# Sixteen row blocks of a down projection by seven block products in place of eight

## Chip, cores, metric

One NeuronCore of a Trainium2 chip runs the whole kernel. The metric is the device time of one execution in microseconds (us); lower is better. Five engines work side by side, each through its own instructions in a fixed order: PE (matrix products), DVE (vector), ACT (scalar and activation), POOL (GpSimd), and SP, which here only issues DMAs. They wait for each other through semaphores.

## What is computed

One layer of a hybrid decoder over 592 columns (16 meta tokens, 512 prompt tokens, 8 sequences of 8 new tokens). A pooling mixer and a state space mixer are merged, projected by w_o and added to x; then comes the channel mixer, which is the part that the change is about:

```python
hn2 = rmsnorm(x, norm2_w)
up, ffn_new = causal_dwconv(hn2 @ w_up, ffn_buf, ffn_conv_w, ffn_conv_b)   # width 3, 5632 columns
x = x + (silu(up[..., :D_FF]) * up[..., D_FF:]) @ w_down                   # D_FF = 2816 = 22 blocks of 128
# then a last rmsnorm of x
```

All of it is float32. Every weight product is made of three matmuls on rounded parts: low weight by high activation, high by high, high by low.

## The kernel before

Activations lie with features on the 128 partitions and tokens in columns. The work is a list of **units**. A unit is one block of 128 output features: it loads a weight block (`load_w`, L87, a DMA on SP into one of two "wr" buffers of 1 MB; one load often serves two units), **splits** it (`split_w`: ACT writes the high part wh at L116, DVE the low part wl at L117, into one of two buffers each, `WBUFS`), does its matmuls (`mm3`, L122 to L124), and ends with a "post" that reads the sums from PSUM. `run` sets the order: after unit u it emits the split of unit u+2, which has to wait for the buffer that unit u has read. A tile scheduler then lays out each engine's instructions in one fixed order by its own costs; within an engine nothing overtakes.

Stages from 580 us on: the merge (units of w_ssd_out, from about 600 us), the output projection (`o_units`; its post sums squares of x2 on POOL and turns the next block of x on PE through an "acc" buffer), the up projection, the down projection, the rest of both. In the up projection the units go gate 0, val 0, gate 1, val 1, ... for j = 0 to 21, 48 matmuls of 290 and 288 columns each. `gate_post` and `val_post` read PSUM (L1157 to L1159), convolve (ACT L1165, DVE L1167 twice), and make tanh (L1179) and its product (L1180) or the product gate times value (L1190), whose high part ACT writes (L1194) and whose low part POOL writes (L1195) into `gh` and `gl`. After j = 11, `down0` multiplies blocks 0 to 11 by w_down: 8 units, two halves of 288 columns, 12 k each, added into x2 by DVE (L1220). After j = 21, `last` does blocks 12 to 21, with the output's transposes between.

Of the kernel before, what the change touches and what calls it, by code (L numbers as in the profile page):

```python
# [8 lines left out]
F32 = mybir.dt.float32  # L9
F32R = mybir.dt.float32r  # L10
# [25 lines left out]
def hybrid_step(  # L36
# [23 lines left out]
    def slot(shape, dt=F32):  # L60
        return sp.tile(shape, dt, tag="T", bufs=9, name=nm("t"))
# [66 lines left out]
    class Unit:  # L128
# [8 lines left out]
        def split(self):  # L137
            if self.ws is None:
                wr = self.raw() if callable(self.raw) else load_w(*self.raw)
                self.ws, k0 = [], 0  # L140
                for kb in self.kbs:
                    w = split_w(wr[:, k0:k0 + kb, self.at:self.at + self.n], kb, self.n, self.spare if kb == 2 else None)
                    self.ws += [(w, k) for k in range(kb)]
                    k0 += kb
                self.pss = []
# [20 lines left out]
        def finish(self):  # L166
# [972 lines left out]
    run(merge[:2] + [ff_params] + merge[2:] + [lambda: xr.extend(load_x(c) for c in range(5))], o_units)  # L1139
    x2s = []  # L1140

    def x2_norm():
        return rnorm(sums["n2"], DM, lambda r, a, b: S.activation(rs2[:, a:b], r, AF.Copy))


    nff, rs2 = slot([128, 18 * 44]), slot([128, NA])

    LF = LP - A0
    WF = LF + 8 * NB
# [2 lines left out]
    def ffn_conv(kb, pss):  # L1152
# [19 lines left out]
        return ap[:, 0:NP], ap[:, 514:594].rearrange("p (b r) -> p b r", b=NB)[:, :, 0:8]  # L1172

    gates = {}
    gh, gl = [], []

    def gate_post(j, pss):
        ext, acc, w = ffn_conv(j, pss)
# [1 line left out]
        V.scalar_tensor_tensor(ext[:, 0:w], ext[:, 0:w], 1.0, acc[:, 0:w], op0=ALU.add, op1=ALU.mult)  # L1180
        gates[j] = ext

    def val_post(j, pss):
        if j % 2 == 0:
            gh.extend(pairs(2, F32R))
            gl.extend(pairs(2, F32R))
        _, acc, w = ffn_conv(NF + j, pss)
        t = gates.pop(j)
        for a, b in zip(parts(t), parts(acc)):
            V.tensor_tensor(a, a, b, ALU.mult)  # L1190
        hi, lo = blk(gh, j)[:, :NY], blk(gl, j)[:, :NY]
        for a, h, l in zip(parts(t), (hi[:, 0:NP], hi[:, NP:].rearrange("p (b j) -> p b j", b=NB)),
                           (lo[:, 0:NP], lo[:, NP:].rearrange("p (b j) -> p b j", b=NB))):
            S.activation(h, a, AF.Copy)  # L1194
            G.tensor_tensor(l, a, f(h), ALU.subtract)  # L1195

    def ff_units(j0, nj):
        out = []
# [120 lines left out]
```

## Time and profile before

| | |
|---|---|
| median of 3 runs | 1229.65 us (1229.41 to 1229.66) |
| profiled execution | 1229.33 us |
| its span, first to last instruction | 1227.6 us |
| mean granted TensorE clock | 0.997 |
| PE busy | 1213.3 us (99%) |
| DVE busy | 778.6 us (63%) |
| ACT busy | 554.3 us (45%) |
| POOL busy | 163.5 us (13%) |

The profile is of one execution. "Busy" of PE counts matmuls that are pipelined, so it says that PE always has work and not that it runs at its peak; whether it waits is read from the chain of waits and from the gaps in the timeline. Clock 1.00 is the full rate.

### The profile page before, as it was taken

The numbers are of one execution on the slowest core, as the hardware profiler recorded it, in microseconds if no ns is written. First come the engines' busy times: TensorE is split into PE (matmuls) and PEld (weight loads), VectorE is DVE, ScalarE is ACT, GpSimd is POOL, SyncE is SP. The second block draws the span as 40 slices with busy tenths as digits, with TensorE's granted clock in tenths as the row PEclk, the third lists the DMA queues.
The fourth block names the chain that finished last, engine by engine and source line by source line (L and its number), as shares of the span: only waits on it lengthen the run. The fifth ranks groups of instructions, "written<-read, shape, count | busy, mean of one in ns | idle before, by whom it ended". The sixth has DMA issues, their size and how long they took to land.

```text
span 1227.6 us, 22630 instructions
## 1 busy us (share of the span) xinstructions
PE 1213.3 (99%) x9159; PEld 1176.5 (96%) x9159; DVE 778.6 (63%) x1378; ACT 554.3 (45%) x1167; POOL 163.5 (13%) x323
## 2 busy tenths in 40 slices
PE   9999999999999999999999999999999999999996
PEld 7999999999999999989999999999999999999996
DVE  6785246668997998886643443477666235667634
ACT  6444443555757567655532223443443112433432
POOL 0340000012012013021100001221212000121100
PEclk9999999999999999999999999999999999999998
DMA  7144425653554545664454432123222223222322
GB/s 213 50 137 128 134 89 181 174 161 80 155 146 124 155 135 154 184 168 118 134 154 123 143 131 98 41 91 96 90 70 78 78 86 104 70 69 91 112 70 77
DMA packets 173432, 144.00 MB, mean 117 GB/s; under 512 B 11622, under 2 KB 162830, under 8 KB 173321
## 3 DMA queue, kind: packets, MB, share of 16 engines
q1 hardware_dynamic: 172865, 142.14, 39.5%
q8 instruction: 72, 1.18, 0.4%
q10 hardware_dynamic: 464, 0.42, 0.1%
q14 instruction: 31, 0.25, 0.1%
HBM read 122.43 MB, written 20.34 MB: 116 GB/s over the span
## 4 chain that ended last, share of the span: by engine, by line
PE 94%; DVE 3%; DMA 1%; issue 1%; ACT 1%; POOL 0%; SPq 0%; DVEq 0%; ACTq 0%; POOLq 0%
PE mm L122 28%; PE mm L123 27%; PE mm L124 27%; PE px L765 2%; PE px L827 1%; PE px L787 1%; PE px L796 1%; PE px L749 1%; DMA wr<-in_w_in_dram 1%; PE px L840 1%; DVE wl L117 1%; PE px L880 1%; PE px L739 0%; DVE ext L561 0%; PE px L122 0%
## 5 line engine op out<-in xcount | busy, mean ns | idle before, releaser
L122 PE MATMUL mm<-s,wl 128*128 128x288 f32 (+4 forms) x2512 | 753.1, 300 | 0.6 <-DVE wl L117 0.6
L123 PE MATMUL mm<-s,wh 128*128 128x288 f32 (+4 forms) x2512 | 746.2, 297 | 0.0
L124 PE MATMUL mm<-s,wh 128*128 128x288 f32 (+4 forms) x2256 | 670.7, 297 | 0.0
L122 PEld LDWEIGHTS mm<-s,wl 128*128 128x128 f32 x2512 | 473.4, 188 | 9.2 <-issue 6.5
L123 PEld LDWEIGHTS mm<-s,wh 128*128 128x128 f32 x2512 | 473.1, 188 | 2.9 <-issue 2.4
L124 PEld LDWEIGHTS mm<-s,wh 128*128 128x128 f32 x2256 | 424.1, 188 | 1.4 <-issue 1.4
L117 DVE TENSOR_TENSOR wl<-wr,wh 128x1024 fp32r<-128x1024 f32 (+1 forms) x164 | 198.2, 1208 | 173.1 <-ACT wh L116 172.7
L116 ACT ACTIVATE wh<-wr 128x1024 fp32r<-128x1024 f32 (+1 forms) x164 | 170.1, 1037 | 236.2 <-PE mm L124 199.0
L124 PE MATMUL mm<-t,wh 128*128 128x290 f32 (+1 forms) x256 | 76.0, 297 | 0.0
L1167 DVE SCALAR_TENSOR_TENSOR acc<-ext,ffT,acc 128x592 f32<-128x592 f32 x88 | 74.2, 844 | 1.7 <-ACT acc L1165 0.2
L663 DVE SCALAR_TENSOR_TENSOR acc<-ext,scT,acc 128x616 f32<-128x616 f32 x72 | 63.8, 887 | 0.4
L737 ACT ACTIVATE t<-t,TK 128x128 f32<-128x128 f32 (+1 forms) x160 | 49.0, 385 | 25.5 <-DVE t L735 25.5
L952 POOL TENSOR_TENSOR sqs<-sqs,acc 128x578 f32<-128x578 f32 x19 | 32.2, 1697 | 142.2 <-ACT acc L951 77.3
L124 PEld LDWEIGHTS mm<-t,wh 128*128 128x128 f32 x256 | 48.2, 188 | 0.0
L1194 ACT ACTIVATE s<-ext 128x512 fp32r<-128x512 f32 (+1 forms) x44 | 17.1, 436 | 64.3 <-DVE ext L1190 64.3
L1158 DVE TENSOR_TENSOR ext<-mm,t 128x224 f32<-128x224 f32 x43 | 16.8, 391 | 41.7 <-PE mm L124 41.7
L1195 POOL TENSOR_TENSOR s<-ext,s 128x512 fp32r<-128x512 f32 (+1 forms) x44 | 37.4, 871 | 34.7 <-ACT s L1194 34.7
L1220 DVE TENSOR_TENSOR t<-t,mm 128x288 f32<-128x288 f32 (+2 forms) x30 | 13.6, 452 | 44.1 <-PE mm L124 43.9
L884 ACT ACTIVATE t<-t,spr 128x128 f32<-128x128 f32 x128 | 40.3, 394 | 1.1 <-PE px L827 1.0
L806 POOL TENSOR_TENSOR s<-s,tmp 128x256 f32<-128x256 f32 (+1 forms) x32 | 31.9, 1018 | 66.9 <-DVE tmp L800 59.1
L1165 ACT ACTIVATE acc<-ext,ffT 128x592 f32<-128x592 f32 x44 | 38.2, 870 | 1.6 <-DVE ext L1159 1.6
L1161 POOL COPY t<-ext 128x18 f32<-128x18 f32 x44 | 11.3, 258 | 203.1 <-DVE ext L1159 203.0
(292 smaller groups left out, 1288.0 us busy)
## 6 DMA issues: line engine op xcount, KB each, us to landing
wr<-in_w_in_dram SPq DMA_DIRECT2D x29, 1024.0 KB
wr<-in_w_up_dram SPq DMA_DIRECT2D x22, 1024.0 KB
t<-in_state_ssm_dram SPq DMA_DIRECT2D x32, 256.0 KB
t<-cumD SPq DMA_DIRECT2D x16, 512.0 KB
out_dram<-t SPq DMA_DIRECT2D x32, 256.0 KB
wr<-in_w_ssd_out_dram SPq DMA_DIRECT2D x8, 1024.0 KB
wr<-in_w_down_dram SPq DMA_DIRECT2D x8, 768.0 KB
wr<-in_w_down_dram SPq DMA_DIRECT2D x8, 640.0 KB
```

Of the source, the lines that this page charges most:

```text
L116: S.activation(wh[:, :kb, :n], wr, AF.Copy)
L117: V.tensor_tensor(wl[:, :kb, :n], wr, f(wh[:, :kb, :n]), ALU.subtract)
L122: PE.matmul(o, wl[:, k, :m], hi[:, a:b], start=first, stop=False)
L123: PE.matmul(o, wh[:, k, :m], hi[:, a:b], start=False, stop=False)
L124: PE.matmul(o, wh[:, k, :m], lo[:, a:b], start=False, stop=last)
L663: V.scalar_tensor_tensor(acc[:, 0:616], ext[:, k:k + 616], scT[:, kb, 24 + k:25 + k], acc[:, 0:616], op0=ALU.mult, op1=ALU.add)
L737: S.activation(seg[:q, h, :q], seg[:q, h, :q], AF.Exp, scale=-1.0, bias=sums_[:, h:h + 1])
L884: S.activation(v[:, b], v[:, b], AF.Copy, scale=elS[:, 4 * u + 2 * i + b, 4 * g + j:4 * g + j + 1])
L952: G.tensor_tensor(sums[key], sums[key], t[:, :NA], ALU.add)
L1165: S.activation(acc[:, 0:w], ext[:, 0:w], AF.Identity, scale=ffT[:, kb, 16:17], bias=ffT[:, kb, 19:20])
L1167: V.scalar_tensor_tensor(acc[:, 0:w], ext[:, k:k + w], ffT[:, kb, 16 + k:17 + k], acc[:, 0:w], op0=ALU.mult, op1=ALU.add)
L1195: G.tensor_tensor(l, a, f(h), ALU.subtract)
```

## The change

Blocks 0 to 7 and 8 to 15 of the down projection are each done as a 2x2 block product with seven products in place of eight (Strassen's scheme in Winograd's form): block k is split even and odd, output blocks in upper and lower four, columns in two halves of 288. Each product has 4 k of 128 rows. The scheme needs four sums of weight quarters, S1 to S4, and four of activations, N1, N2, T3 and T4.

- The weight sums are made in DRAM: per set four copies of 1 MB on SP's queue (`copies`) and seven adding DMAs of 1 MB on POOL's queue (`adds`). Each is tied by `held_back` to the weight split that was emitted last, so that it does not start before.
- The activation sums are made on DVE in `val_post` of every odd j under 16, and split; the low parts of the new sums on DVE, the others on POOL.
- `Two` is a unit of two products with a split of 512 elements each; `Parts` loads four weight quarters into one wr buffer. 14 units for each set: four column pairs (mp), seven products each.
- The order is now gate and val 0 to 7, gate 8, the first sevens, val 8 to val 15, gate 16, the second sevens, the rest to j = 21, and `last` over blocks 16 to 21. The small state DMAs come two units later.

```diff
-        V.tensor_tensor(wl[:, :kb, :n], wr, f(wh[:, :kb, :n]), ALU.subtract)
+        split_done.append(V.tensor_tensor(wl[:, :kb, :n], wr, f(wh[:, :kb, :n]), ALU.subtract))
...
+    SEVEN = (("A11", "B11"), ("A12", "B21"), ("S4", "B22"), ("S2", "N2"), ("S1", "N1"), ("S3", "T3"), ("A22", "T4"))
+
+    def held_back(dma):
+        tc.add_manual_dep(dma.ins, split_done[-1].ins.name,
+                          mybir.DependencyInfo(mybir.DependencyClass.Sync, mybir.DependencyReason.DATA),
+                          reason="its time has not come")
...
+        def copy(self, s, a):
+            return lambda: held_back(DMA.dma_start(out=self.d[s], in_=self.at[a]))
+        def add(self, s, a):
+            return lambda: held_back(G.dma_start(out=self.d[s], in_=self.at[a], accum_op=ALU.add))
+        def copies(self):
+            return [self.copy("S4", "A12"), self.copy("S2", "A11"), self.copy("S1", "A21"), self.copy("S3", "A11")]
+        def adds(self):
+            return [self.add("S4", "A11"), self.add("S2", "A21"), self.add("S1", "A22"), self.add("S4", "A21"), self.add("S3", "A21"),
+                    self.add("S2", "A22"), self.add("S4", "A22")]
...
+    class Parts:
+        def load(self):
+            if self.of is None:
+                raws.clear()
+                self.of = wp.tile([128, 4, 4, 128], F32, tag="wr", bufs=2, name=nm("wr"))
+                for i, v in enumerate(self.views):
+                    DMA.dma_start(out=self.of[:, i], in_=v)
...
+    class Two(Unit):
+        def split(self):
+            if self.ws is None:
+                self.ws = []
+                wh = wp.tile([128, 2, 4, 128], F32R, tag="wh", bufs=WBUFS, name=nm("wh"))
+                wl = wp.tile([128, 2, 4, 128], F32R, tag="wl", bufs=WBUFS, name=nm("wl"))
+                for i, (parts, at, *_) in enumerate(self.prods):
+                    src, n = parts.get(at), 4
+                    S.activation(wh[:, i, :n], src, AF.Copy)
+                    split_done.append(V.tensor_tensor(wl[:, i, :n], src, f(wh[:, i, :n]), ALU.subtract))
+                    self.ws.append(((wh[:, i], wl[:, i]), n))
...
+    def placed(units, steps):
+        return [x for i, u in enumerate(units) for x in [u, *steps.get(i, ())]]
...
+    run(merge[:2] + [ff_params] + placed(merge[2:], {0: d0.copies()[0:2], 1: d0.copies()[2:4], 2: d0.adds()[0:1], 4: d0.adds()[1:2]}) + [lambda: xr.extend(load_x(c) for c in range(5))], o_units)
...
+    def split_g(hi, lo, src, eng):
+        S.activation(hi, src, AF.Copy)
+        eng.tensor_tensor(lo, src, f(hi), ALU.subtract)
...
+        split_g(gB[p][0][:, 0:2], gB[p][1][:, 0:2], qd[:, 2:4], G)
+        V.tensor_tensor(n1, qd[:, 0], qd[:, 1], ALU.subtract)
+        V.scalar_tensor_tensor(n2, n1, -1.0, qd[:, 3], op0=ALU.mult, op1=ALU.subtract)
+        V.tensor_tensor(t3, qd[:, 3], qd[:, 1], ALU.subtract)
+        V.scalar_tensor_tensor(t4, n2, -1.0, qd[:, 2], op0=ALU.mult, op1=ALU.subtract)
+        split_g(gB[p][0][:, 2:4], gB[p][1][:, 2:4], t[:, 0:2 * NH].rearrange("p (h t) -> p h t", h=2), V)
+        split_g(gB[p][2][:, 1], gB[p][2][:, 3], t3, V)
+        i = 2 * (p % 2)
+        split_g(gB[p][3][:, i], gB[p][3][:, i + 1], t4, V)
...
+        if w == "A11":
+            u = held["u"] = acc_tile()[:, :NH]
+            S.activation(u, p, AF.Copy)
+            to(0, p, ALU.add)
+        elif w == "S2":
+            u = held["u"]
+            V.tensor_tensor(u, u, p, ALU.add)
+            to(2, u, ALU.subtract)
+        elif w == "S1":
+            u = held.pop("u")
+            V.tensor_tensor(u, u, p, ALU.add)
+            to(1, u, ALU.add)
+            to(3, u, ALU.subtract)
...
-    up = ff_units(0, 12)
+    up = ff_units(0, 8)
     x_turn(0)
-    run(o_units, up)
+    run(placed(o_units, {0: d0.adds()[2:3], 4: d0.adds()[3:4]}), up)
...
-    down0 = down_units(0, [6, 6], GHALF)
-    last = down_units(12, [8, 2], LAST)
+    up2, up3 = ff_units(8, 8), ff_units(16, 6)
+    last = down_units([5, 1], LAST)
...
-    seq = up + down0 + ff_units(12, 10) + [out_begin, last[0]]
+    seq = (placed(up, {0: d0.adds()[4:5], 4: d0.adds()[5:6], 8: d0.adds()[6:7], 9: d1.copies()[0:2], 10: d1.copies()[2:4], 12: d1.adds()[0:1]})
+           + up2[:1] + placed(down_sevens(0), {1: d1.adds()[1:2], 9: d1.adds()[2:3]})
+           + placed(up2[1:], {1: d1.adds()[3:4], 4: d1.adds()[4:5], 7: d1.adds()[5:6], 10: d1.adds()[6:7]}) + up3[:1] + down_sevens(1) + up3[1:]
+           + [out_begin, last[0]])
     for m in range(1, 6):
-        seq += [last[m], *([ff_states] if m == 2 else []), lambda m=m: out_block(0, m - 1), lambda m=m: out_block(1, m - 1)]
+        seq += [last[m], *([ff_states] if m == 4 else []), lambda m=m: out_block(0, m - 1), lambda m=m: out_block(1, m - 1)]
```

**Merge, SP's queue.** Each row is a DMA; w0S are the four sums of the first set, wr_8171 (before: wr_8159) is the second to last block of w_ssd_out. Before:

```order
L1076 DMA ext_8389<-mAD 128x578 [waits DMAHW3_49,DMAHW2_49,DVE_49]
L95 DMA wr_8159<-in_w_ssd_out_dram 128x16x128 [waits DVE_49]
L1077 DMA acc_8390<-tbD 128x578 [waits DMAHW4_49,DVE_49]
L1076 DMA ext_8505<-mAD 128x578 [waits DMAHW6_49,DMAHW5_49,DVE_49]
L95 DMA wr_8279<-in_w_ssd_out_dram 128x16x128 [waits DVE_49]
```

After:

```order
L1183 DMA ext_8402<-mAD 128x578 [waits DMAHW3_49,DMAHW2_49,DVE_49]
L201 DMA w0S_7485<-in_w_down_dram 512x1x512 [waits DVE_49]
L201 DMA w0S_7483<-in_w_down_dram 512x1x512 [waits DMAHW4_49]
L201 DMA w0S_7482<-in_w_down_dram 512x1x512 [waits DMAHW5_49,DVE_49]
L201 DMA w0S_7484<-in_w_down_dram 512x1x512 [waits DMAHW6_49]
L95 DMA wr_8171<-in_w_ssd_out_dram 128x16x128 [waits DMAHW7_49,Activation_49]
L95 DMA wr_8292<-in_w_ssd_out_dram 128x16x128 [waits DMAHW0_49,Activation_49]
```

The four copies stand ahead of the last two loads of the merge, and the loads of tbD and mAD blocks that stood between those now come behind.

**Up projection, DVE's queue, about the unit val 6.** wl is the low part of a weight split, ext and acc the buffers of a post. Before, in this stage (gate and val take turns with this pattern):

```order
L1158 TENSOR_TENSOR ext_9401<-mm_9352,t_8534 128x224 [waits PE_49]
L1180 SCALAR_TENSOR_TENSOR ext_9333<-ext_9333,acc_9339 128x592 [waits Activation_49]
L1159 TENSOR_TENSOR ext_9401<-mm_9352,t_8534 128x8x8
L117 TENSOR_TENSOR wl_9420<-wr_9417,wh_9419 128x1024 [waits DMAHW4_49,Activation_49]
L1167 SCALAR_TENSOR_TENSOR acc_9407<-ext_9401,ffT,acc_9407 128x592 [waits Activation_49]
L1167 SCALAR_TENSOR_TENSOR acc_9407<-ext_9401,ffT,acc_9407 128x592 [waits DVE_49]
```

After, where wl_10025 is the split of val 6 and ext_10078 belongs to gate 6, the unit ahead of it:

```order
L1270 TENSOR_TENSOR ext_10078<-mm_10029,sqs_9201 128x8x8
L1278 SCALAR_TENSOR_TENSOR acc_10084<-ext_10078,ffT,acc_10084 128x592 [waits Activation_49]
L1278 SCALAR_TENSOR_TENSOR acc_10084<-ext_10078,ffT,acc_10084 128x592 [waits DVE_49]
L1290 SCALAR_TENSOR_TENSOR ext_10078<-ext_10078,acc_10084 128x592 [waits Activation_49]
L117 TENSOR_TENSOR wl_10025<-wr_10022,wh_10024 128x1024 [waits DMAHW0_49,Activation_49]
L117 TENSOR_TENSOR wl_10091<-wr_9940,wh_10090 128x1024 [waits Activation_49]
```

The split stood behind the PSUM reads of the unit two before its own, and stands now behind the last PSUM read, the convolution and the tanh product of the unit just before its own; the split of the unit after follows at once.

**Up projection to first sevens, DVE's queue.** Before, at the end of val 11, where `down0` begins (wl_10814 is one of its splits):

```order
L1159 TENSOR_TENSOR ext_10795<-mm_10746,t_8534 128x8x8
L117 TENSOR_TENSOR wl_10742<-wr_10735,wh_10741 128x768 [waits Activation_49]
L1167 SCALAR_TENSOR_TENSOR acc_10801<-ext_10795,ffT,acc_10801 128x592 [waits Activation_49]
L1167 SCALAR_TENSOR_TENSOR acc_10801<-ext_10795,ffT,acc_10801 128x592 [waits DVE_49]
L1190 TENSOR_TENSOR ext_10723<-ext_10723,acc_10801 128x512 [waits DVE_49]
L1190 TENSOR_TENSOR ext_10723<-ext_10723,acc_10801 128x8x8
L117 TENSOR_TENSOR wl_10814<-wr_10811,wh_10813 128x768 [waits DMAHW6_49,Activation_49]
L1220 TENSOR_TENSOR t_7478<-t_7478,mm_10821 128x288 [waits PE_49]
```

After, where wl_10310 and wl_10388 are the splits of the first four products, ext_10375 belongs to gate 8 and acc_10291 to val 7:

```order
L251 TENSOR_TENSOR wl_10310<-wr_10311,wh_10309 128x512 [waits DMAHW3_49,Activation_49]
L251 TENSOR_TENSOR wl_10388<-wr_10311,wh_10387 128x512 [waits DMAHW4_49,Activation_49]
L251 TENSOR_TENSOR wl_10388<-wr_10311,wh_10387 128x512 [waits DMAHW5_49,Activation_49]
L1268 TENSOR_TENSOR ext_10375<-mm_10325,sqs_9201 128x290 [waits Pool_49]
L1269 TENSOR_TENSOR ext_10375<-mm_10326,sqs_9201 128x224 [waits PE_49]
L1270 TENSOR_TENSOR ext_10375<-mm_10326,sqs_9201 128x8x8
L1290 SCALAR_TENSOR_TENSOR ext_10217<-ext_10217,acc_10223 128x592 [waits Activation_49]
L1278 SCALAR_TENSOR_TENSOR acc_10291<-ext_10285,ffT,acc_10291 128x592 [waits Activation_49]
L1278 SCALAR_TENSOR_TENSOR acc_10381<-ext_10375,ffT,acc_10381 128x592 [waits Activation_49]
L1278 SCALAR_TENSOR_TENSOR acc_10291<-ext_10285,ffT,acc_10291 128x592 [waits DVE_49]
L1278 SCALAR_TENSOR_TENSOR acc_10381<-ext_10375,ffT,acc_10381 128x592 [waits DVE_49]
L1321 TENSOR_TENSOR t_10155<-ext_10217,acc_10291 128x512 [waits DVE_49]
```

Both splits of the second pair now stand ahead of gate 8's PSUM reads and of val 7's convolution, product and sums; eleven more rows (sums, low parts, two adds from PSUM) follow before wl_10424, the split for S1 and S3.

## Rows read from the trace of the kernel before

**Rows 1.** The page, part 1: busy us (share of the span) xinstructions.

```profile
PE 1213.3 (99%) x9159; PEld 1176.5 (96%) x9159; DVE 778.6 (63%) x1378; ACT 554.3 (45%) x1167; POOL 163.5 (13%) x323
```

**Rows 2.** The page, part 4: shares of the chain that ended last, by engine.

```profile
PE 94%; DVE 3%; DMA 1%; issue 1%; ACT 1%; POOL 0%; SPq 0%; DVEq 0%; ACTq 0%; POOLq 0%
```

**Rows 3.** Waits of PE over the run: us in total, times, longest us.

```profile
PE mm L122 <- DVE wl L117: 0.6, 2, 0.4
```

**Rows 4.** Windows: stretch, length, busy us (x instructions) per engine, PEclk, DMA share, GB/s.

```profile
580.00:700.00 120.00, 120.00 (x914) 118.40 (x913) 57.16 (x90) 41.30 (x71) 5.95 (x6) 1.00 0.49 141
...
788.00:932.00 144.00, 144.00 (x1085) 144.00 (x1084) 98.47 (x168) 60.26 (x82) 29.18 (x63) 1.00 0.25 79
...
932.00:1008.00 76.00, 76.00 (x575) 76.00 (x573) 30.23 (x45) 17.41 (x24) 6.88 (x10) 1.00 0.30 87
...
1140.00:1215.00 75.00, 75.00 (x567) 74.08 (x566) 37.21 (x91) 29.39 (x107) 3.87 (x6) 1.00 0.25 73
```

**Rows 5.** Timeline of DVE at a unit's end: start us, us, engine, operation.

```profile
905.57 0.39 DVE L1158 TENSOR_TENSOR ext<-mm,t 128x224 f32<-128x224 f32 x1 [0.85 <-PE mm L124]
905.87 0.21 DVE L1159 TENSOR_TENSOR ext<-mm,t 128x64 f32<-128x64 f32 x1
906.66 1.23 DVE L117 TENSOR_TENSOR wl<-wr,wh 128x1024 fp32r<-128x1024 f32 x1 [0.57 <-ACT wh L116]
...
911.97 0.39 DVE L1158 TENSOR_TENSOR ext<-mm,t 128x224 f32<-128x224 f32 x1 [1.36 <-PE mm L124]
```

**Rows 6.** Timeline of ACT, columns as Rows 5, merge and 905 us.

```profile
688.25 1.06 ACT L116 ACTIVATE wh<-wr 128x1024 fp32r<-128x1024 f32 x1 [5.03 <-issue]
...
694.67 1.06 ACT L116 ACTIVATE wh<-wr 128x1024 fp32r<-128x1024 f32 x1 [1.82 <-PE mm L124]
...
905.57 1.06 ACT L116 ACTIVATE wh<-wr 128x1024 fp32r<-128x1024 f32 x1 [1.66 <-PE mm L124]
```

**Rows 7.** Groups by line and shape, 788 to 1160 us: busy us, mean ns.

```profile
L1167 DVE SCALAR_TENSOR_TENSOR acc<-ext,ffT,acc 128x592 f32<-128x592 f32 x88 | 74.2, 844 | 1.7 <-ACT acc L1165 0.2
...
L117 DVE TENSOR_TENSOR wl<-wr,wh 128x1024 fp32r<-128x1024 f32 x46 | 56.5, 1227 | 32.8 <-ACT wh L116 32.5
...
L116 ACT ACTIVATE wh<-wr 128x1024 fp32r<-128x1024 f32 x46 | 48.7, 1059 | 65.8 <-PE mm L124 60.9 <-PE px L124 4.8
...
L1165 ACT ACTIVATE acc<-ext,ffT 128x592 f32<-128x592 f32 x44 | 38.2, 870 | 1.6 <-DVE ext L1159 1.6
...
L1157 DVE TENSOR_TENSOR ext<-mm,t 128x290 f32<-128x290 f32 x43 | 19.5, 453 | 0.9 <-PE mm L124 0.9
...
L1180 DVE SCALAR_TENSOR_TENSOR ext<-ext,acc 128x592 f32<-128x592 f32 x22 | 17.1, 777 | 10.5 <-ACT ext L1179 10.4
...
L1179 ACT ACTIVATE ext<-acc 128x592 f32<-128x592 f32 x22 | 15.4, 699 | 48.0 <-DVE acc L1167 45.5 <-DVE ext L1157 2.5
...
L1190 DVE TENSOR_TENSOR ext<-ext,acc 128x512 f32<-128x512 f32 x22 | 15.0, 682 | 0.1
...
L1194 ACT ACTIVATE s<-ext 128x512 fp32r<-128x512 f32 x22 | 13.9, 632 | 64.3 <-DVE ext L1190 64.3
...
L1220 DVE TENSOR_TENSOR t<-t,mm 128x288 f32<-128x288 f32 x16 | 7.3, 454 | 19.0 <-PE mm L124 18.8
```

**Rows 8.** Timeline of SP in the merge, columns as Rows 5.

```profile
684.18 0.38 SPq L95 DMA_DIRECT2D wr<-in_w_ssd_out_dram  x1
```

**Rows 9.** The page, part 3: queue: packets, MB, share of 16 engines.

```profile
q1 hardware_dynamic: 172865, 142.14, 39.5%
```

**Rows 10.** Timeline of PE at the program's end, columns as Rows 5.

```profile
1218.14 0.44 PE L1234 MATMUL px<-ident,t 128*128 128x128 f32 x2 [0.30 <-DVE t L1220]
```

**Rows 11.** Windows at the program's end, columns as Rows 4.

```profile
1220.00:1221.00 1.00, 0.00 (x0) 0.00 (x0) 0.79 (x5) 0.17 (x2) 0.00 (x0) 1.00 0.00 0
1221.00:1222.00 1.00, 0.00 (x0) 0.00 (x0) 1.00 (x3) 0.59 (x1) 0.00 (x0) 0.65 0.00 0
1222.00:1223.00 1.00, 0.00 (x0) 0.00 (x0) 0.15 (x1) 0.00 (x0) 0.00 (x0) 0.50 0.43 172
```

More of the change, by code (lines that the diff above doesn't have):

```diff
@@ L141, in split @@
                 for kb in self.kbs:
[L142 removed]
+                    w = split_w(wr[:, k0:k0 + kb, self.at:self.at + self.n], kb, self.n, self.spare if kb <= 2 else None)
                     self.ws += [(w, k) for k in range(kb)]
@@ new lines, in hybrid_step, with __init__, get @@
+    class Parts:
+        def __init__(self, views):
+            self.views, self.of, self.nxt = views, None, None
+        def load(self):
[4 more added lines that the diff above has]
+                    DMA.dma_start(out=self.of[:, i], in_=v)
+        def get(self, i):
+            self.load()
+            if self.nxt:
+                self.nxt.load()
+            return self.of[:, i]
@@ new lines, in hybrid_step, with __init__, product, finish @@
+    class Two(Unit):
+        def __init__(self, prods):
+            Unit.__init__(self, None, 0, None, None, None, None)
+            self.prods = prods
+        def split(self):
[8 more added lines that the diff above has]
+                    self.ws.append(((wh[:, i], wl[:, i]), n))
+        def product(self, halves=None, piece=None):
+            for (_, _, acts, post), (w, n) in zip(self.prods, self.ws):
+                ps = px_tile()
+                for k in range(n):
+                    act = acts(k)
+                    n2 = act[0].shape[1]
+                    mm3(ps[:, :n2], w, k, 128, act, 0, n2, k == 0, k == n - 1)
+                post(ps)
+        def finish(self):
+            for fn in due:
+                fn()
+            due.clear()
+            now = pend[:]
+            pend.clear()
+            due[:0] = [fn() for fn in now]
@@ new lines, in seven_units @@
+    def seven_units(sums, mps, acts, post):
+        todo = [(mp, w, x) for mp in mps for w, x in SEVEN]
+        parts = [Parts([sums.view(w, mp) for mp, w, _ in todo[i:i + 4]]) for i in range(0, len(todo), 4)]
+        for a, b in zip(parts, parts[1:]):
+            a.nxt = b
+        prods = [(parts[i // 4], i % 4, lambda k, x=x: acts(k)[x], lambda ps, mp=mp, w=w: post(mp, w, ps))
+                 for i, (mp, w, x) in enumerate(todo)]
+        return [Two(prods[i:i + 2]) for i in range(0, len(prods), 2)]
@@ L1138, in hybrid_step @@
     o_units[0].k_outer = True
-    run(merge[:2] + [ff_params] + merge[2:] + [lambda: xr.extend(load_x(c) for c in range(5))], o_units)
-    x2s = []
+    dsum = [Sums(w_dn_m, 8 * i, f"w{i}") for i in range(2)]
+    d0, d1 = dsum
+    run(merge[:2] + [ff_params] + placed(merge[2:], {0: d0.copies()[0:2], 1: d0.copies()[2:4], 2: d0.adds()[0:1], 4: d0.adds()[1:2]}) + [lambda: xr.extend(load_x(c) for c in range(5))], o_units)
+    x2s, rs2 = [], []
     def x2_norm():
-        return rnorm(sums["n2"], DM, lambda r, a, b: S.activation(rs2[:, a:b], r, AF.Copy))
-    nff, rs2 = slot([128, 18 * 44]), slot([128, NA])
+        spread = rnorm(sums["n2"], DM, lambda r, a, b: S.activation(rs2[0][:, a:b], r, AF.Copy))
+        rs2.append(ep.tile([128, NA], F32, tag="sqs", bufs=1, name=nm("sqs")))
+        return spread
+    nff = slot([128, 18 * 44])
     LF = LP - A0
@@ L1181, in gate_post @@
         gates[j] = ext
+    NH = NY // 2
+    gB, quad = {}, {}
+    gh, gl = [], []
+    def split_g(hi, lo, src, eng):
+        S.activation(hi, src, AF.Copy)
+        eng.tensor_tensor(lo, src, f(hi), ALU.subtract)
     def val_post(j, pss):
-        if j % 2 == 0:
-            gh.extend(pairs(2, F32R))
-            gl.extend(pairs(2, F32R))
         _, acc, w = ffn_conv(NF + j, pss)
-        t = gates.pop(j)
-        for a, b in zip(parts(t), parts(acc)):
-            V.tensor_tensor(a, a, b, ALU.mult)
@@ L1191, in val_post @@
[L1191 to L1195, printed above, removed]
+        t, p, e = gates.pop(j), j // 2, j % 2
+        if j >= 16:
+            if e == 0:
+                gh.extend(pairs(2, F32R))
+                gl.extend(pairs(2, F32R))
+            for a, b in zip(parts(t), parts(acc)):
+                V.tensor_tensor(a, a, b, ALU.mult)
+            hi, lo = blk(gh, j - 16)[:, :NY], blk(gl, j - 16)[:, :NY]
+            for a, h, l in zip(parts(t), (hi[:, 0:NP], hi[:, NP:].rearrange("p (b j) -> p b j", b=NB)),
+                               (lo[:, 0:NP], lo[:, NP:].rearrange("p (b j) -> p b j", b=NB))):
+                S.activation(h, a, AF.Copy)
+                G.tensor_tensor(l, a, f(h), ALU.subtract)
+            return
@@ new lines, in val_post @@
+        if e == 0:
+            quad[p] = slot([128, 4, NH])
+        qd = quad[p]
+        g = qd[:, 2 * e:2 * e + 2].rearrange("p h t -> p (h t)")
+        for o, a, b in zip((g[:, 0:NP], g[:, NP:].rearrange("p (b j) -> p b j", b=NB)), parts(t), parts(acc)):
+            V.tensor_tensor(o, a, b, ALU.mult)
+        if e == 0:
+            new = slot if p % 4 == 3 else big
+            gB[p] = [new([128, 4, NH], F32R), new([128, 4, NH], F32R), big([128, 4, NH], F32R),
+                     gB[p - 1][3] if p % 2 else big([128, 4, NH], F32R)]
+            split_g(gB[p][2][:, 0], gB[p][2][:, 2], qd[:, 0], G)
+            return
```

43 lines of the change are left out of this document (36 added, 7 removed).

## The prediction

> **What bounds the kernel now.** I read four views. The first part of the page [rows 1] gives PE 99% of the span; busy PE is not PE at its peak, so I went on to the chain that ended last [rows 2], 94% of which is PE, and to what PE waited for [rows 3]: for a weight split (L117) only 0.6 us in the whole run. The windows [rows 4] show where other engines have room: from 580 us to 1215 us PE is busy all the time, while DVE is busy 48% in the merge (57.16 of 120 us), 68% in the first up projection (98.47 of 144), 40% in the down projection of block rows 0 to 11 (30.23 of 76) and 50% at the end. So the time goes by the number of matmuls, and a matmul that is taken away is time gained, as long as nothing else ends last. The timeline shows why PE never waits now: at a unit's end (905.57, 911.97) ACT starts the high part of a weight [rows 6], DVE the low part 1.09 us later, done 2.3 us after the unit's end [rows 5], and that weight belongs to the unit after next, so it is there some 4 us early. Two such ends lie 6.40 us apart, for 48 matmuls: 0.1333 us each.
>
> **The change, part by part.** The profiled execution took 1229.33 us (span 1227.6); the median of the three runs is 0.3 us above that. I sum against 1229.33 and add 0.3 at the end.
>
> *Matmuls.* Eight row blocks times eight column blocks as a 2x2 block product: 4 k x 7 products x 3 matmuls for each of 4 column pairs in place of 4 x 8 x 3. For both sets that is 672 matmuls of 288 columns where there were 768. 96 x 0.1333 = **-12.8 us**. By itself 1216.5.
>
> Everything else is about whether PE then waits. I go through the places in the order of time. Durations of single operations are those of [rows 7] (line numbers of before; in the changed file L1165, L1167, L1179, L1180 and L1190 are L1276, L1278, L1289, L1290 and L1321); a split of 512 elements has no row, and I take 0.63 on ACT (L1194, same size) and 0.69 on DVE (L1190, same size).
>
> *Merge.* SP now issues four copies of 1 MB from DRAM to DRAM ahead of the load of the second to last w_ssd_out block. That load was issued at 684.18 [rows 8] and its split ran at 694.67 [rows 6]: 10.5 us of lead, and some 4 us more until PE needs it. A copy has no row. 142.14 MB in 39.5% of the span [rows 9] is 293 GB/s, or 3.6 us for 1 MB, if a copy costs as much as a load; twice that, if its reads and writes add up. Two copies may start at 684.2 and end at 691.4; the other two are held until the split that starts at 688.25 on ACT [rows 6] and is done at 690.5, so they end at 698.6, and the load behind them at 702.2. The latest start of the split that costs nothing is 694.67 + 4 = 698.7: 3.5 us late. Ends 0 and 10; taken: **+4**.
>
> *Output projection.* The fourth adding DMA of the first set stands in POOL's queue ahead of the square sums of x2 and waits for a split. Those sums release the acc buffer that the next transposes and the next o_post need, so PE's banks come free later. The split is done 2.3 us after a unit's end [rows 5], and the order gives the rest of that chain (square sum, transposed x, o_post) about as much again before PE gets a bank. Issuing an adding DMA has no row; the nearest is an issue on SP, 0.38 us [rows 8]. Ends 0 and 5; taken: **+3**.
>
> *Pairs.* Every second val of the first 16 now makes four more 288-column operations (4 x 0.45) and splits of 576, 288 and 288 columns on DVE. Per pair of j (four units, 25.6 us of PE) DVE has 17.5 us now (98.47 of 144 [rows 4]); 1.8 for the sums and 0.8 + 2 x 0.45 for the splits make it 21. It still fits, so the price is only a weight split that comes late behind a burst: ends 0 and 6 over the eight pairs, taken **+2**.
>
> *val6.* This is the first sure place. Before, each split stands right behind the bank reads of the unit two before its own. Now the split of val6 stands behind the whole of gate6, the unit just before val6: bank reads, two L1278, tanh, L1290. From gate6's end: 0.2 (last read) + 0.87 (ACT, L1165) + 2 x 0.84 + 0.70 (tanh) + 1.06 (high part; L1290's 0.78 beside it) + 1.23 (low part) and five hops of 0.03 between engines (906.63 to 906.66 [rows 5, 6]): **5.9 us in which PE has nothing**, since the next matmul needs this weight. That is the lower end. DVE comes to this place with the sums of val5 behind it, and its queue is then 2 to 4 us late. The reason for the order is the load: it stands behind the four copies of the second set, two of them held until the split of gate6, about 2.5 us after gate5's end. Two copies and the load at 3.6 land 13.3 us after gate5's end, gate6 ends 12.8 after it, so the load is about as late as the order makes it; with copies at 7.2 it lands at 20.5 and the stall is 10 to 14, with DVE's 4 on top 18. Ends 5.9 and 18; taken: **+8**.
>
> *Start of the first sevens.* The second sure place. On ACT and DVE the split of the second pair of products stands ahead of the whole of val7's work and waits for the weight buffer of gate8. Count from val7's end: gate8 ends at 6.4; two splits until 8.5; then three bank reads, L1290, four L1278, two L1321, four sums, another L1290, a PSUM add and three subtractions, at 0.45 to 0.84 each, to 19.7; then the split for S1, at 20.4. PE has gate8 (6.4) and four products of 1.6 us, then needs S1, at 12.8. Stall 7.6 by this count; operations of one engine overlap by some 0.08 us (905.57 and 905.87 [rows 5]), which takes 1.2 off, and late copies add. Ends 4 and 9; taken: **+7.5**.
>
> *Within the sevens.* Per column pair PE has 84 matmuls, 11.2 us; DVE 11 adds of 0.454 and 7 splits of 0.69, 9.8 us; ACT 5. DVE is at 88% and still ahead: 0, up to 4 over eight column pairs if hops cost 0.1 us for each of 18 operations.
>
> *Start of the second sevens.* Here the splits of val15's successors are mixed with its work, not all ahead of it. The same count gives S2 1.1 us, S1 and S3 some 0.7 us late: ends 0 and 5, taken **+2**.
>
> *Clock.* PE's last matmul before its end started at 1218.14 and took 0.44 [rows 10]; the granted clock was 1.00 until 1221, 0.65 in the next microsecond and 0.50 after [rows 11]. When it fell to the lower level (1.2 GHz) PE had done nothing since 1218.6. Two of the stalls above, perhaps four, leave PE idle longer than that. The trace has no row of the way back: each microsecond of matmuls at the lower level costs half a microsecond, and as an estimate I take 1.5 us for each of the two sure ones, as if the clock were as slow to rise as it was to fall. Ends 0 and 8; taken: **+3**. The Trainium skill ("TensorE: Matmul & The Clock Gate", Part 1: The HAM clock gate) says that an idle array's clock is gated to half rate. By that the clock term is not 0 at any stall that is long enough; the trace agrees on the way down and shows nothing of the way up.
>
> *Last stage.* Six row blocks in place of ten: units of 36 matmuls (4.8 us) with about 3.9 us of DVE and 3.4 of ACT. The state DMAs moved by two units end well before the output. 0.
>
> Sum: -12.8 + 4 + 3 + 2 + 8 + 7.5 + 2 + 3 = **+16.7**: 1246.0, with 0.3 for the median **1246.3 us**, 1.4% slower.
>
> **The rivals.**
>
> *A, faster or no change: the buffers give it all back.* The sure places stay, but at their lower ends (5.9 + 4), and merge, output projection, pairs and second sevens find their cover: the 4 us by which each split is early now [rows 5, 6] swallow each of these. Then 1216.8 + 9.9 = 1226.7, or up to 1230 with the clock. It decides for faster if both stalls together stay under about 10.3 us (12.8 less the 2.5 us, 0.2%, that a measurement of this kernel can tell from no change). For it: four of six terms are only bounded, with zero as an end. Against it: the 5.9 us follow from one order on three engines, and nothing of PE lies beside them.
>
> *B, much slower: the DMAs collide.* The copies move 8 MB and the adding DMAs 14 MB that are new, and if each costs 7.2 us per MB, merge comes to +8, val6 to +16, and the loads of the first sevens, which have about 7 us of window for 1 MB, wait behind the second set's adds, +5. With the other terms as above, 1246.3 + 4 + 8 + 5 = 1263. For it: the queue [rows 9] is already 0.25 to 0.49 busy [rows 4]. Against: the adds are spread over 60 units. The Trainium skill ("DMA: Bandwidth & Descriptors", Issuing engines are not separate DMA queues) says that DMAs from SP and GpSimd run on the same 16 engines and interleave. By that POOL's adds slow SP's loads, which is B; the trace of before has no DMA from POOL to show it.
>
> *C, DVE bounds the sevens.* If adds and splits take 10% more than their rows, DVE has 11.7 us per column pair where PE has 11.2: +4, 1250. It lies in the forecast's own range.
>
> **How the numbers follow.** Forecast with its terms, C among them (1236 to 1257): 0.60. A: 0.23, half of it faster, half within 0.2%. B: 0.17. The forecast's own range is 1236 to 1257; to hold 8 in 10 the range goes into A and B: 1228 to 1266. Faster by over 0.2%: 0.12; within: 0.11; slower: 0.77.
>
> **What would show it.** In the profile after, PE's idle time should be 25 to 32 us, in two large pieces: one before val6's first matmul, put down to the split L117, and one in the first sevens before S1, put down to the split L251. The merge's stall shows on L117 after a late load, that of the output projection on DVE's o_post. The granted clock should fall at these places. Matmul pace between them stays 0.133 us. It is wrong if PE's idle time is under 10 us (A), or if ACT's high part waits for a DMA in most units of the sevens (B).

## The result, and the profile after

The changed kernel took 1384.92 us (median; 1384.12 to 1387.28) against 1229.66 us before: ratio 1.1265, 95% interval 1.1245 to 1.1284. Slower was forecast, 1246.3 us with a range up to 1266; the loss is 155.3 us where 16.7 were expected.

The page of the profile after, its parts 1, 2 and 4 (columns as in [rows 1] and [rows 2]):

```profile
PE 1235.9 (89%) x9063; PEld 1192.1 (86%) x9063; DVE 852.8 (62%) x1546; ACT 580.6 (42%) x1223; POOL 202.6 (15%) x321
...
PEclk9999999999999999999978998895988899899998
...
PE 68%; DMA 16%; DVE 11%; ACT 2%; issue 2%; SPq 2%; POOL 0%; DVEq 0%; ACTq 0%; POOLq 0%
```

There are 96 matmuls fewer, as counted. But PE is 68% of the chain that ended last, where it was 94% [rows 2], and 16% is DMA, which was 1%. The granted clock, below full before in the last of the 40 slices only, falls in nine others as well. What PE waited for (us in total, times, longest us) answers to [rows 3], where a weight split cost 0.6 us in all:

```profile
PE mm L122 <- DVE wl L117: 84.1, 9, 35.0
PE mm L122 <- DVE ext L1268: 21.2, 4, 11.5
PE px L122 <- DVE wl L251: 11.5, 6, 4.6
PE px L1224 <- DMA t<-in_x_prompt_dram: 5.3, 3, 3.6
PE mm L122 <- ACT s L1238: 4.4, 1, 4.4
PE px L122 <- ACT t L1298: 3.9, 1, 3.9
```

The releaser named is DVE's low part of a split, but DVE itself waited. The long pieces of the chain say for what (start us, us, what):

```profile
709.80 22.54 DMA wr<-in_w_ssd_out_dram
...
946.30 21.48 DMA wr<-in_w_up_dram
...
1148.42 17.72 DMA wr<-in_w_up_dram
```

These are loads of 1 MB, each 18 to 22 us from the start of its issue to landing. At the 293 GB/s of [rows 9] such a load takes 3.6 us. The largest stall is the one before val 6. SP's timeline there, then the first ACT and PE instructions behind the load (start us, us):

```profile
920.53 25.66 SPq L201 DMA_DIRECT2D w1S<-in_w_down_dram  x4
946.30 10.04 SPq L95 DMA_DIRECT2D wr<-in_w_up_dram  x1
```

```profile
967.86 2.00 ACT L116 ACTIVATE wh<-wr 128x1024 fp32r<-128x1024 f32 x2 [24.26 <-DMA wr<-in_w_up_dram]
```

```profile
970.32 0.58 PE L122 MATMUL mm<-s,wl 128*128 128x290 f32 x1 [34.99 <-DVE wl L117]
```

PE did nothing from 935 to 970 us. The four copies were issued between 920.5 and 946.2, the load behind them at 946.3, and it landed at 967.8. SP was held 10.04 us in the issue of that load alone (the issue of a load took 0.38 us in [rows 8]), so half of the wait passed before the load was on its way. What the DMA engines did meanwhile stands in the windows (columns as in [rows 4]; the last two numbers are the mean busy share of the 16 DMA engines and GB/s):

```profile
946.00:956.00 10.00, 0.00 (x0) 0.00 (x0) 0.00 (x0) 0.00 (x0) 0.00 (x0) 0.50 0.26 102
1135.50:1138.00 2.50, 2.50 (x21) 2.50 (x20) 2.13 (x5) 1.71 (x4) 0.49 (x1) 1.00 0.28 52
1154.00:1165.00 11.00, 7.53 (x57) 7.30 (x55) 3.23 (x8) 1.03 (x2) 2.99 (x4) 0.99 0.28 58
```

In the first, copies alone are under way: a share of 0.26 of 16 engines is four engines, and 102 GB/s makes 10.3 us of a copy of 1 MB. That it is four engines all the time, and not 16 a quarter of it, the trace's single packets show: of its 2 KB packets four are under way at a time (five or six where one ends as the next begins), and each takes 0.084 us. In the second, one add alone: again 0.28, 52 GB/s, 20 us for 1 MB. In the third, a load is awaited (it was issued at 1148.4 and landed at 1166.1) beside an add, and still only 0.28 of the engines work: twelve of them have done their part, and the load's last quarter shares four engines with the add (211 packets of the add and 207 of the load ran in that window). So the first theory: **copies and adds run on four of the 16 engines, and the weight loads wait for those four.** The shape would be the reason: both name the four blocks first and the 128 rows of a block second. The Trainium skill ("DMA: Bandwidth & Descriptors", Why a DMA increments its semaphore by 16 and not by 1) says that the number of engines is the largest divisor, up to 16, of the slowest dimension's size on both sides; a slowest dimension of four gives four, and the trace agrees with 0.26 x 16 = 4.2. The Trainium skill says on the same page (Rules for kernel authors) to put outermost a dimension whose size is a multiple of 16, at best the 128 partitions.

By place, PE's waits in the profile after against the terms of the prediction:

| place | predicted us | waited us |
|---|---|---|
| merge | 4 | 26.5 |
| output projection | 3 | 10.2 |
| first up projection before val 6 (pairs) | 2 with the later ones | 10.6 |
| val 6 | 8 | 35.0 |
| first sevens | 7.5 | 15.4 |
| up projection between the sevens | no term of its own | 32.3 |
| second sevens | 2 | 0.9 |

That is 130.9 us. PE is also busy 32.5 us longer than in a kernel below with the same 9063 matmuls and almost no stalls (1235.9 against 1203.4): that is the lower clock behind the stalls (in the trace PE is busy 62.5 us at a granted clock of 0.50, and none of its time in that kernel). 130.9 + 32.5 - 12.8 = 150.6 of the 155.3 us. Of the rest, 2.9 us are matmul time that was counted and not gained: PE is busy 1203.4 us there and 1213.3 before, 9.9 us less and not 12.8.

### The profile page after: what moved, and what is told of

Its sections match the earlier page's. It is cut to its first block, busy times and chain, and to the rows that moved or that the text cites. A ratio compares the mean times of both kernels' runs of the same rounds, so it can differ in the third digit from the quotient of the medians.

```text
span 1383.6 us, 22872 instructions
## 1 busy us (share of the span) xinstructions
PE 1235.9 (89%) x9063; PEld 1192.1 (86%) x9063; DVE 852.8 (62%) x1546; ACT 580.6 (42%) x1223; POOL 202.6 (15%) x321
## 4 chain that ended last, share of the span: by engine, by line
PE 68%; DMA 16%; DVE 11%; ACT 2%; issue 2%; SPq 2%; POOL 0%; DVEq 0%; ACTq 0%; POOLq 0%
PE mm L122 18%; PE mm L124 17%; PE mm L123 17%; DMA wr<-in_w_up_dram 9%; DMA wr<-w0S 3%; DVE wl L117 2%; PE px L122 2%; PE px L124 2%; PE px L123 2%; DMA wr<-in_w_ssd_out_dram 2%; DVE acc L1278 2%; SPq L201 2%; PE px L872 1%; ACT wh L116 1%; PE px L934 1%
## 5 line engine op out<-in xcount | busy, mean ns | idle before, releaser
L122 PE MATMUL mm<-s,wl 128*128 128x290 f32 (+4 forms) x2278 | 693.7, 305 | 109.9 <-DVE wl L117 84.1
L123 PE MATMUL mm<-s,wh 128*128 128x290 f32 (+4 forms) x2278 | 685.2, 301 | 0.0
L124 PE MATMUL mm<-s,wh 128*128 128x290 f32 (+3 forms) x2022 | 608.5, 301 | 0.5 <-DVE s L1239 0.5
L122 PEld LDWEIGHTS mm<-s,wl 128*128 128x128 f32 x2278 | 437.1, 192 | 121.5 <-issue 63.3
L123 PEld LDWEIGHTS mm<-s,wh 128*128 128x128 f32 x2278 | 436.7, 192 | 2.9 <-issue 2.4
L124 PEld LDWEIGHTS mm<-s,wh 128*128 128x128 f32 x2022 | 387.2, 192 | 2.2 <-issue 1.4
L122 PE MATMUL px<-s,wl 128*128 128x288 f32 (+4 forms) x234 | 73.7, 315 | 11.5 <-DVE wl L251 11.5
L123 PE MATMUL px<-s,wh 128*128 128x288 f32 (+4 forms) x234 | 72.0, 308 | 0.0
L124 PE MATMUL px<-s,wh 128*128 128x288 f32 (+4 forms) x234 | 71.9, 308 | 0.0
L844 ACT ACTIVATE t<-t,TK 128x128 f32<-128x128 f32 (+1 forms) x160 | 49.0, 384 | 26.3 <-DVE t L842 26.3
L122 PEld LDWEIGHTS px<-s,wl 128*128 128x128 f32 x234 | 46.7, 199 | 13.5 <-DVE wl L251 13.1
L251 DVE TENSOR_TENSOR wl<-wr,wh 128x512 fp32r<-128x512 f32 x56 | 37.0, 685 | 22.8 <-ACT wh L250 22.6
L124 PEld LDWEIGHTS px<-s,wh 128*128 128x128 f32 x234 | 46.7, 200 | 0.3 <-DVE s L418 0.3
```

The source lines that it names most:

```text
L122: PE.matmul(o, wl[:, k, :m], hi[:, a:b], start=first, stop=False)
L123: PE.matmul(o, wh[:, k, :m], hi[:, a:b], start=False, stop=False)
L124: PE.matmul(o, wh[:, k, :m], lo[:, a:b], start=False, stop=last)
L251: split_done.append(V.tensor_tensor(wl[:, i, :n], src, f(wh[:, i, :n]), ALU.subtract))
L844: S.activation(seg[:q, h, :q], seg[:q, h, :q], AF.Exp, scale=-1.0, bias=sums_[:, h:h + 1])
```

## Experiments

Rivals of the theory: traffic from DRAM to DRAM is slow however it is cut; the adds on POOL's own queue do not touch the loads; or the order of the work on DVE and ACT, on which the prediction was built, costs most of it. Ratios are to the kernel before, timed beside.

**All copies and adds over 16 engines.** The same bytes, with the row first:

```diff
-            return lambda: held_back(DMA.dma_start(out=self.d[s], in_=self.at[a]))
+            return lambda: held_back(DMA.dma_start(out=self.d[s].rearrange("k p c -> p k c"), in_=self.at[a].rearrange("k p c -> p k c")))
...
-            return lambda: held_back(G.dma_start(out=self.d[s], in_=self.at[a], accum_op=ALU.add))
+            return lambda: held_back(G.dma_start(out=self.d[s].rearrange("k p c -> p k c"), in_=self.at[a].rearrange("k p c -> p k c"), accum_op=ALU.add))
```

> The changed kernel with one edit: copies and adding DMAs name the 128 rows of a block first and the four blocks second, so that each is cut over 16 DMA engines and not over four. The same bytes go to the same places. Theory (each copy and each add runs on four engines, a copy takes 10 us, an add 20 and more, and the loads queued behind them come late): copies of 3 to 4 us, adds of 5 to 8 us, PE idle after 690 us falls from 137 us to under 25, time 1222 to 1245 us. Rival (traffic from DRAM to DRAM is slow in itself, however it is cut): copies stay near 10 us, time above 1350 us.

Measured: 1226.45 us, ratio 0.9969 (0.9956 to 0.9983). One edit of the DMAs' shape takes 158.5 us away and turns the change into a gain of 0.3%. PE's waits for a weight split, and two microseconds of the merge in which copies alone are under way:

```profile
PE mm L122 <- DVE wl L117: 4.5, 4, 3.6
```

```profile
688.00:690.00 2.00, 2.00 (x17) 2.00 (x16) 0.61 (x1) 1.06 (x1) 0.00 (x0) 1.00 1.05 386
```

The share is 1.05 (packets of one engine overlap a little) and the rate 386 GB/s in place of 0.26 and 102: 16 or a few more packets are under way at a time, and one still takes 0.084 us. The page's rows on the adds (median us to landing) are, after and with this edit:

```profile
w0S<-in_w_down_dram POOLq DMA_DIRECT2D x7, 1024.0 KB, 28.5
```

```profile
w0S<-in_w_down_dram POOLq DMA_DIRECT2D x7, 1024.0 KB, 11.4
```

From its first packet to its last a copy takes 10.3 to 11.4 us after and 3.4 to 4.3 with this edit, an add 20.4 to 26.2 and 6.2 to 9.1; I had expected 3 to 4 and 5 to 8. So DRAM to DRAM is not slow in itself. One reservation: the scheduler lays out the instructions by its own costs, the DMAs' shape among them, and with this edit it also puts the split of val 6 back behind the unit two before it. The edit therefore takes away the order that the prediction spoke of, too; the last experiment puts that back alone. The splits at the start of the first sevens are laid out otherwise as well, and that order was not put back.

**Copies alone, adds alone.** The first line of the edit without the second, and the second without the first.

> Only the copies are cut over 16 engines; the adds stay on four. Theory: the two largest stalls (26.8 us in the merge, 35.3 us before val 6) belong to the copies and go to under 6 us each, and the clock's loss behind them with them; the stalls in the second part of the up projection, which lie beside adds, stay: 1310 to 1330 us. Rival (the adds alone make the loads late): 1370 us or more.

> Only the adds are cut over 16 engines; the copies stay on four. Theory: the stalls of the merge and before val 6 stay (27 and 35 us), the load waits in the second part of the up projection (10.0, 3.1, 7.4 and 11.8 us) and those of the first sevens mostly go: 1315 to 1345 us. Rival (adds run on POOL's own queue and do not touch the loads): 1375 us or more.

Measured: 1349.3 us with the copies cut over 16 engines, 1287.2 with the adds, one run each. So the larger part lies on the adds: undoing their four engines alone gives 98 us, undoing the copies' alone 36, both 158. The scheduler's order goes along here too: with the copies cut, the split of val 6 is back behind the unit two before it; with the adds cut, it stays late, and the second pair of splits in the first sevens no longer stands ahead of val 7's work, so that some of the 98 us can be that order (7.5 us by the prediction). I had expected 40 to 70 us from the adds and 55 to 75 from the copies (1315 to 1345 and 1310 to 1330 us in time); both missed, in opposite directions, since I had put the first stalls of the up projection and those of the output projection down to the copies. PE's waits with the adds cut over 16 engines, over the run (the longest is the one before val 6), and in the merge:

```profile
PE mm L122 <- DVE wl L117: 63.3, 4, 36.1
```

```profile
PE mm L122 <- DVE wl L117: 26.3, 1, 26.3
```

The two stalls of the copies (26.3 and 36.1 us; 26.5 and 35.0 after) are there almost unchanged, and the others are gone but for pieces under 2 us. With the copies cut over 16 engines, on the other hand, the merge waits for nothing, and 16.4 us are left before val 6, beside an add:

```profile
PE mm L122 <- DVE wl L117: 16.4, 1, 16.4
```

That the two parts alone give 133 and not 158 fits this in part: before val 6 the load is late for either reason, and what one edit takes away there the other reason keeps. The wait there is 35.0 us after, 16.4 with the copies cut, 36.1 with the adds cut and 3.6 with both, so 13.9 of the missing 25 us are this. Where the other 11 went was not worked out; with the copies alone cut, the waits beside adds grew (in the output projection 13.1 us in place of 10.2).

**Without the weight sums.** Copies and adds left out, quarters of w_down read in the place of S1 to S4:

```diff
-            return lambda: held_back(DMA.dma_start(out=self.d[s], in_=self.at[a]))
+            return lambda: None
...
-            return lambda: held_back(G.dma_start(out=self.d[s], in_=self.at[a], accum_op=ALU.add))
+            return lambda: None
...
-            full = self.d[name] if name in self.d else self.at[name]
+            full = self.at[{"S1": "A21", "S2": "A11", "S3": "A12", "S4": "A22"}.get(name, name)]
```

> The weight sums are left out: no copies, no adds, and the products that should read S1 to S4 read a quarter of w_down in their place, so that all matmuls, splits, loads and activation sums stay. It shows what is left of the change without its DMAs. Theory (the DMAs are all of the loss): 1217 to 1224 us, that is the gain of the matmuls less small waits. Rival (the order of the work on DVE and ACT costs what the prediction said, 7.5 us at the sevens and 2 for the pairs): 1228 to 1240 us.

Measured: 1219.27 us, ratio 0.9906 (0.9878 to 0.9935), 10.9 us under the kernel before beside it. The matmuls' gain is real (1216.5 was the count without waits), and seven products, their sums on DVE and their splits cost at most 3 us of waits. PE's waits for the splits of the sevens there:

```profile
PE px L122 <- DVE wl L251: 1.1, 2, 0.6
```

The DMAs were the whole loss, together with the order that the scheduler lays out on their account: without them the split of val 6 stands behind the unit two before it again.

**Other places for the second set's copies.** In the version over 16 engines 3.6 us were left before val 6, where a load stood between the two pairs of copies:

```diff
-    ... 9: d1.copies()[0:2], 10: d1.copies()[2:4], 12: d1.adds()[0:1]})
+    ... 7: d1.copies()[0:2], 11: d1.copies()[2:4], 12: d1.adds()[0:1]})
```

> The version cut over 16 engines, with the second set's copies emitted after units 7 and 11 of the up projection in place of 9 and 10, so that each pair of copies stands right behind a weight load on SP's queue and not ahead of one. Theory (what is left there, 3.9 us of idle PE before val 6 and the slower clock behind it, is a load that stands behind copies): that gap goes, 1220 to 1223 us. Rival (the load is late for lack of DMA rate, wherever the copies stand): no change, 1225 to 1228 us.

Measured: 1221.25 us, ratio 0.9931 (0.9917 to 0.9945): the fastest complete version, 8.7 us under the kernel before beside it. Its page (part 1) and what is left of PE's waits for splits in the sevens:

```profile
PE 1203.4 (99%) x9063; PEld 1165.5 (95%) x9063; DVE 850.3 (70%) x1546; ACT 580.8 (48%) x1223; POOL 189.9 (16%) x321
```

```profile
PE px L122 <- DVE wl L251: 1.6, 3, 0.6
```

SP's queue in the version over 16 engines, and here:

```profile
858.69 1.32 SPq L201 DMA_DIRECT2D w1S<-in_w_down_dram  x2
860.11 0.63 SPq L95 DMA_DIRECT2D wr<-in_w_up_dram  x1
864.33 4.88 SPq L201 DMA_DIRECT2D w1S<-in_w_down_dram  x2
```

```profile
845.45 1.28 SPq L201 DMA_DIRECT2D w1S<-in_w_down_dram  x2
853.97 5.42 SPq L95 DMA_DIRECT2D wr<-in_w_up_dram  x2
870.48 1.24 SPq L201 DMA_DIRECT2D w1S<-in_w_down_dram  x2
```

Each pair of copies now has a load of w_up ahead of it and some 8 us until the next one, and the wait before val 6 is gone.

**No hold.** In the version over 16 engines, `held_back` returns the DMA without its dependency:

```diff
-        tc.add_manual_dep(dma.ins, split_done[-1].ins.name,
-                          mybir.DependencyInfo(mybir.DependencyClass.Sync, mybir.DependencyReason.DATA),
-                          reason="its time has not come")
+        return dma
```

> The version cut over 16 engines, without the hold: copies and adds wait for nothing but their own data. In the order they then all stand in the first stage, eight copies ahead of the third and fourth load of w_in. Theory (a DMA costs PE time only when a load waits behind it): a stall of 10 to 30 us in the first 100 us and nothing at the later places, 1230 to 1250 us. Rival (it does not matter where DMAs stand once they use all engines): 1219 to 1224 us.

Measured: 1280.96 us, one run. Worse than either expected: the eight copies are now issued from 25 to 69 us and the adds from 37 us on, ahead of loads of w_in and pool_w that the next work needs, and PE waits there:

```profile
PE px L588 <- DVE t L576: 38.5, 1, 38.5
PE mm L122 <- ACT ext L652: 9.2, 1, 9.2
PE mm L122 <- DVE wl L117: 5.8, 2, 5.4
```

So the DMAs have to be held back even where they use all engines; the hold was not what failed in the change, the shape was. I had expected 10 to 30 us of stall there and it is 53.5.

**The late split by itself.** On the fastest version, the split of val 6 is made to wait for gate 6's last operation on DVE, which is the order of the changed kernel on DVE:

```diff
-        S.activation(wh[:, :kb, :n], wr, AF.Copy)
+        hi = S.activation(wh[:, :kb, :n], wr, AF.Copy)
+        if behind:
+            tc.add_manual_dep(hi.ins, behind.pop().ins.name, ...)
...
+                if late_units and units[i - 1] is late_units[0]:
+                    behind.append(gate_ops[-1])
+                    late_units.pop().split()
...
+    late_units.append(up[13])
```

> As e5_places, with one wait added: the split of val 6 stands behind gate 6's last operation on DVE, as in the changed kernel, while all DMAs are cut over 16 engines. It measures by itself the term of the prediction that was called sure. Prediction's count: PE idle 5.9 us before val 6, more with a late queue, and 1.5 us of clock: e5_places plus 6 to 10 us, 1227 to 1232. Rival (the term was wrong too, the wait is hidden): within 1.5 us of e5_places.

Measured: 1234.79 us, ratio 1.0035 (1.0022 to 1.0048), 13.5 us over the version without that wait. PE's wait there, DVE's timeline and four windows (the eighth number is the granted clock):

```profile
PE mm L127 <- DVE wl L122: 10.1, 1, 10.1
```

```profile
877.33 0.21 DVE L1278 TENSOR_TENSOR ext<-mm,sqs 128x64 f32<-128x64 f32 x1
878.49 1.70 DVE L1286 SCALAR_TENSOR_TENSOR acc<-ext,ffT,acc 128x592 f32<-128x592 f32 x2 [0.95 <-ACT acc L1284]
881.03 0.78 DVE L1298 SCALAR_TENSOR_TENSOR ext<-ext,acc 128x592 f32<-128x592 f32 x1 [0.84 <-ACT ext L1297]
882.98 1.23 DVE L122 TENSOR_TENSOR wl<-wr,wh 128x1024 fp32r<-128x1024 f32 x1 [1.17 <-ACT wh L117]
```

```profile
876.00:877.00 1.00, 0.00 (x0) 0.00 (x0) 1.00 (x4) 0.18 (x1) 0.27 (x1) 0.84 0.22 79
877.00:878.00 1.00, 0.00 (x0) 0.00 (x0) 0.54 (x3) 0.43 (x1) 0.31 (x2) 0.50 0.14 50
...
884.00:888.00 4.00, 3.65 (x15) 3.68 (x16) 0.21 (x1) 0.00 (x0) 1.25 (x1) 0.50 0.38 38
...
891.00:892.00 1.00, 1.00 (x10) 1.00 (x9) 0.00 (x0) 0.00 (x0) 0.00 (x0) 1.00 1.12 207
```

The chain is the one that was counted: last read, convolution, tanh, product, high part, low part, 6.9 us from 877.33 to 884.2 (with the high part behind the product here, not beside it). The read itself came 3.1 us after the end of gate 6's last matmul (874.2), because DVE was still at the sums of val 5. After the stall the clock is at 0.50, and 24 matmuls run at the lower level, 1.2 GHz, until 890.3, one each 0.242 us. They take 5.9 us in place of 3.2, 2.7 us more. 10.1 + 2.7 = 12.8 of the 13.5 us.

## Why the prediction was wrong

**Right, a little too large: the matmuls.** 96 fewer, and 1219.27 us with the weight sums left out, against 1216.5 counted without any wait: 10.9 us gained against the kernel beside it, of 12.8.

**Right in kind and size: the late split.** 5.9 us with nothing for PE, and 2 to 4 us more for a late queue: 10.1 measured when it was put back alone (about 1 us of it because the high part, too, stood behind the product there). In the changed kernel it cannot be seen, since the load behind the copies came later still.

**Wrong, the first half of the step that failed: the price of a copy.** "142.14 MB in 39.5% of the span is 293 GB/s, or 3.6 us for 1 MB, if a copy costs as much as a load; twice that, if its reads and writes add up." Both ends took for granted that a DMA uses all 16 engines. A copy took 10.3 us and an add 20, on four. The merge came to 26.5 us in place of 4, val 6 to 35.0 in place of 8 (or 18 at its upper end). The order of SP's queue prints a copy as 512x1x512, where each load has 128 first; that the slowest dimension of its source is four blocks stands only in the code, and I did not ask what it does to the engines.

**Wrong, the other half: the adds had no term.** Beside loads they stood in the sum with nothing, in rival B with 5 us. They are the larger part: 98 us went when they alone were cut over 16 engines, with an unknown part of it from the order that the scheduler changed along with them. An add of 20 us on four engines makes a quarter of every load beside it late (17.7 us in place of 3.6), and the 14 adds lie beside most of the loads from the output projection to the second sevens. "Against: the adds are spread over 60 units" was taken as a point against B, and it was what spread the harm. Rival B had the mechanism, loads that wait for copies and adds, at less than a quarter of its size: its terms of 8, 16 and 5 us stand against 130.9 us of waits. The sign that was named for it, ACT's high part waiting for a DMA in most units of the sevens, looked at the wrong place. ACT waited far more for loads of the up projection than for the sums in the sevens (14.9 us in four times):

```profile
ACT wh L116 <- DMA wr<-in_w_up_dram: 110.0, 10, 24.3
```

**Mis-sized: the clock.** The way down was read rightly: when the late split was put back, the clock read 0.84 in the microsecond from 876 and 0.50 from 877, with no matmul since 874.2. The way back, for which there was no row, cost 2.7 us after the one stall that was put back alone, where 1.5 was estimated, and after is 32.5 us in all, since there were a dozen stalls and not two.

**Not settled: the start of the first sevens.** 7.5 us were expected from the order on ACT and DVE. After, 15.4 us were waited there, but with adds beside it; in the versions over 16 engines the scheduler chose another order, and no more than 1.6 us is left. The wait of that order with fast DMAs was not measured.

**A slip in rival C.** Adds and splits that take 10% more make 10.8 us per column pair of 9.8 and not 11.7, which is still under PE's 11.2: as it was stated, C would have cost nothing. In the fastest version 1.6 us of waits for these splits are left over the whole run.

## What to carry to other kernels

Price a DMA by the engines it can use, and read that from its access pattern before its bytes: the mean busy share of the 16 engines in a window where it runs alone tells it at once (0.26 here for four). A DMA on few engines is not only slow itself: every load that is cut over all engines waits for its own part on those few (17.7 us beside an add here), and a DMA queued behind it on the same issuing engine waits as well (10.04 us in its issue alone). Where copies have to share a queue with loads that are just in time, emit them right behind a load and not ahead of one: that was worth some 5 us here.

## What the runs showed of the hardware beside that

In each of the eight pairs with activation sums, one DVE operation of 288 columns takes 1.7 us where the others of its kind take 0.45. It is the first that starts after POOL has begun a low part of 576 columns, and it ends 0.3 us after POOL does. From the fastest version, DVE and POOL (start us, us):

```profile
823.24 0.45 DVE L1334 TENSOR_TENSOR t<-t 128x288 f32<-128x288 f32 x1
823.61 1.70 DVE L1335 SCALAR_TENSOR_TENSOR acc<-ext,t 128x288 f32<-128x288 f32 x1
```

```profile
823.27 1.73 POOL L1299 TENSOR_TENSOR s<-t,s 128x576 fp32r<-128x576 f32 x1 [1.55 <-ACT s L1298]
```

The Trainium skill ("SBUF — State Buffer", Who interferes with whom) says that a DVE instruction with two inputs from SBUF contends with a GpSimd instruction that reads SBUF; the trace agrees here, with 1.25 us of DVE in each pair. That it goes by POOL's start and not by the line shows in the version over 16 engines, in the one pair where DVE is an operation less far when POOL begins:

```profile
878.80 1.67 DVE L1334 TENSOR_TENSOR t<-t 128x288 f32<-128x288 f32 x1
880.40 0.45 DVE L1335 SCALAR_TENSOR_TENSOR acc<-ext,t 128x288 f32<-128x288 f32 x1
```

```profile
878.58 1.58 POOL L1299 TENSOR_TENSOR s<-t,s 128x576 fp32r<-128x576 f32 x1 [7.60 <-ACT s L1298]
```

No experiment took POOL's operation away, so the cause is argued and not shown. It is not seen to cost PE time in the fastest version, whose waits for splits come to 1.8 us.
